# An attention layer on one Trainium2 core: sums of squares of four heads in fp32 in the array's column groups, roots on transposed sums, and two value chunks behind the first score blocks

## The chip, the cores and the metric

The kernel runs on one core of one Trainium2 chip. The core has five engines that matter here: TensorE, a 128 x 128 array for matrix products, written PE (its loads of stationary weights are shown apart, as PEld); VectorE, DVE; ScalarE, ACT; GpSimd, POOL; and SyncE, SP, which issues the DMAs. Matrix products are accumulated in PSUM, a memory of eight banks of 128 partitions x 512 fp32 numbers; everything else lies in SBUF.

The metric is device time in microseconds (us) of one execution, as the median of several runs.

## What is computed

The reference is a backbone of two layers over 512 latent tokens (width 1024) and 256 context tokens, in fp32. Layer 0 mixes with a gated convolution, layer 1 with attention; around each mixer stands a SwiGLU half step. The change is inside the attention mixer. Cut to it:

```python
D_MODEL, SEQ, CTX_LEN, HEAD_DIM = 1024, 512, 256, 128
N_HEADS, N_KV_HEADS, Q_BLOCK, NORM_EPS = 8, 2, 128, 1e-6

def rms_norm(x, g):
    return x * lax.rsqrt(jnp.mean(x * x, axis=-1, keepdims=True) + NORM_EPS) * g

def project_qkv(h, w_qkv, q_g, k_g):
    qkv = h @ w_qkv                      # 8 q heads, 2 k heads, 2 v heads
    ...
    return rms_norm(q, q_g), rms_norm(k, k_g), v

def gqa_block(q, k, v):
    s = jnp.einsum('bqkgd,bskd->bkgqs', q, k) * (HEAD_DIM ** -0.5)
    return jnp.einsum('bkgqs,bskd->bqkgd', jax.nn.softmax(s, axis=-1), v)

def attention_mixer(h_lat, h_ctx, ...):
    q_l, k_l, v_l = project_qkv(h_lat, w_qkv, q_g, k_g)
    q_c, k_c, v_c = project_qkv(h_ctx, w_qkv, q_g, k_g)
    q_l, k_l = apply_rope_2d(q_l, cos, sin), apply_rope_2d(k_l, cos, sin)
    k_all, v_all = concat(k_c, k_l), concat(v_c, v_l)     # 768 keys
    o_l = ...gqa_block over blocks of 128 queries...
    return o_l @ w_o
```

For every q head the kernel needs, per token, the root of the mean of 128 squares. Since this factor is the same for all keys, it isn't multiplied into q but given to the exponential of the softmax as its scale (rq), and to the row's maximum with a minus sign (nrq).

## The kernel before

**Products.** Activations lie transposed, features on partitions and tokens along the free dimension. An fp32 product is made of three products in a reduced type (fp32r): a number is split into a high part, a copy made by ACT, and a low part, the difference made by DVE (split, L179 to L181); mm3 (L808 to L811) forms high times high, high times low and low times high into one PSUM bank. Weights arrive by DMA as raw tiles and are split in the same way (w<-raw at L180 and L181), well ahead of their use; w_get takes the next split weights, w_done gives the space of those used back.

**Projections.** attention (from L1314) projects the heads one after the other. p is the projected head in PSUM (bank tag A, for head 2 tag B). A head's work behind its projection comes in two steps: q_head or k_head issues ACT's and DVE's part, and the function post that it returns issues the PE part, which is put into the middle of a later projection (behind, and the loop over the value chunks). For a q head (L1362) ACT squares p into hs; parts_of (L616 to L620) forms th, an ACT copy with epsilon added, and tl, the DVE difference; turned applies the rotary tables; post (L1369, L1370) multiplies pick, a matrix of zeros with one column of ones, with th and tl, so that the sum over the 128 partitions lands in row h of the 8 x 512 tile ps_Q. For a k head parts_of is followed by rstd_of, whose sums are broadcast over all partitions (ps_S).

**Value chunks.** Then six chunks of 128 tokens are multiplied by the v weights (loop over sc, L1423 to L1437), 24 products each, into one of two B banks; ACT copies the high parts vh and DVE forms the low parts vl, for each of the two kv heads g. Behind chunk 3 the 8 x 512 tile of sums gets its reciprocal root (rsqrt, L605 to L612: logarithm and exponential on ACT, one refinement step on DVE). Behind chunk 5 four transposes turn it into 128 x 32 (ps_S), and DVE writes rq and nrq.

**The block loop.** PSUM is then given out anew: C, two tiles of two banks each, for scores, T for transposes, O for the output. For each of 8 heads and 4 blocks of 128 queries: scores forms a 128 x 768 tile ps_C (six products), DVE its row maximum and the bias sm, ACT the exponential pr with its row sum, DVE the reciprocal, and the scaling of pr is done by DVE (even blocks) or ACT (odd blocks). turn makes six 128 x 128 transposes of pr, in two trios with a T tile each; ACT copies a trio into the high part of p and DVE forms the low part. values multiplies two blocks' p with the values into ps_O, which is split into o. The loop runs scores two blocks ahead of turn, and values one step behind. After block 15 T is given two banks instead of three, and one bank goes to the output projection of heads 0 to 3, whose steps (filler) fill the rest of the loop.

**What sets the order.** PE and SP run their instructions in the order in which the code issues them. For ACT and DVE a scheduler chooses the order when the program is built; on the chip each engine runs its instructions one by one in that order. Tiles of one tag share a ring of buffers: a new tile waits until the tile that held its buffer has been read for the last time.

Of the kernel before, what the change touches and what calls it, by code (L numbers as in the profile page):

```python
# [9 lines left out]
F32 = mybir.dt.float32  # L10
# [111 lines left out]
def backbone(ctx: ExitStack, tc: tile.TileContext, a: dict, out: bass.AP):  # L122
# [8 lines left out]
    def ctile(name, shape, dt=F32):  # L131
        return const.tile(shape, dt, name=name, tag=name)
# [13 lines left out]
    def ptile(name, shape=(P, 512)):  # L146
        pool, tag = bank[name]
        return pool.tile(list(shape), F32, name=f"ps_{name}", tag=tag)
# [13 lines left out]
    q_g, k_g = vec["attn_q_g"], vec["attn_k_g"]  # L162
    ones_r = ctile("ones_r", [P, P], F32R)
    dve.memset(ones_r.bitcast(F32), 1.0)
    pick = ctile("pick", [P, 2 * HEADS], F32R)
    dve.memset(pick.bitcast(F32), 0.0)
    dve.memset(pick[:, HEADS : HEADS + 1].bitcast(F32), 1.0)
    eps_t = {}
    for dim in (D, HD):
        eps_t[dim] = ctile(f"eps{dim}", [P, 1])  # L170
# [5 lines left out]
    def slot(n, shape, name, dt=F32R):  # L176
        return xp.tile([P, *shape], dt, name=name, tag=f"T{n}")
# [1140 lines left out]
    def attention(gp, i, s, after):  # L1318
# [7 lines left out]
        make_identity(nc, ident)  # L1326
        part_tiles[:] = (gp, "th"), (gp, "tl")

        with tc.tile_pool(name="rope", bufs=1) as rp, psum(A=4, B=2, S=1, Q=1):
            rope_c = rp.tile([P, NL], F32, name="rope_c", tag="rope_c")  # L1330
            rope_s = rp.tile([P, NL], F32, name="rope_s", tag="rope_s")
            pq = ptile("Q", (HEADS, NL))

            def turned(dst, p, g, n):

# [24 lines left out]
                return post  # L1360

            def q_head(p, h):  # L1362
                t = tmp.tile([P, NL], F32, name="hs", tag="t")
                act.activation(t, p, AF.Square)
                th, tl = parts_of(t, NL, HD)
                turned(qf[h], p, q_g, NL)

                def post():
                    pe.matmul(pq, pick[:, HEADS - h : 2 * HEADS - h], th, start=(h == 0), stop=False)  # L1369
                    pe.matmul(pq, pick[:, HEADS - h : 2 * HEADS - h], tl, start=False, stop=(h == HEADS - 1))  # L1370

                return post

# [46 lines left out]
            for h in range(3, HEADS):  # L1420
                q_project(h, 2 if 4 <= h < 7 else 1)
            wv = [w_get() for _ in range(4)]
            for sc in range(6):  # L1423
                post = heads.pop(0)() if heads else None
                p = ptile("B", (P, 2, 256))[:, 0, :]
                ts = slice(sc * P, (sc + 1) * P)
                for k in range(KC):
                    if post and k == KC // 2:
                        post()
                    wvh, wvl = (t[:, 2 * (k % 2) : 2 * (k % 2) + 2, :] for t in wv[k // 2])  # L1430
                    pe.matmul(p, hh[k][:, ts], wvh, start=(k == 0), stop=False)
                    pe.matmul(p, hl[k][:, ts], wvh, start=False, stop=False)
                    pe.matmul(p, hh[k][:, ts], wvl, start=False, stop=(k == KC - 1))
                for g in range(KVH):
                    pg = p[:, g * HD : (g + 1) * HD]
                    act.activation(vh[g][:, sc, :], pg, AF.Copy)
                    dve.tensor_tensor(out=vl[g][:, sc, :], in0=pg, in1=vh[g][:, sc, :].bitcast(F32), op=ALU.subtract)  # L1437
                if sc == 3:
                    r8 = tmp.tile([P, NL], F32, name="r8", tag="r", bufs=2)[:HEADS, :]
                    rsqrt(r8, pq, HEADS, NL, HD)  # L1440
            w_done()
            pt = ptile("S", (P, 4, HEADS))
            for b in range(4):
                pe.transpose(pt[:, b, :], r8[:, b * P : (b + 1) * P], ident[:HEADS, :HEADS])
            dve.tensor_scalar_mul(rq, pt, isq)
            dve.tensor_scalar_mul(nrq, pt, -isq)

        def o_tiles(g):

            got = []  # L1450
            for n in ((4, 5, 8), (11, 12, 13))[g]:
                t = slot(n, [3, NL], f"o{n}")
                got += [t[:, c, :] for c in range(3)]
            return got[:4], got[4:8]

        with tc.tile_pool(name="core", bufs=2) as cp, psum(C=2, O=1), ExitStack() as more:
            more.enter_context(psum(T=3))
            gates.append(lambda: gate_vec(i, s, False))
            st = {}

# [51 lines left out]
                split(oh[h % 4][:, hs], ol[h % 4][:, hs], p)  # L1512

            blocks = [(h, blk) for h in range(HEADS) for blk in range(4)]
            ready = [scores(*blocks[0]), scores(*blocks[1])]
            late = None
            filler = iter(())
            for n, (h, blk) in enumerate(blocks):
                if n + 2 < len(blocks):
                    ready.append(scores(*blocks[n + 2]))  # L1520
                p = turn(h, blk, ready[n])
                ready[n] = None
                if late:
                    values(*late)
                    if late[:2] == (3, 1):
                        more.close()
                        more.enter_context(psum(T=2, AB=1))
                        filler = out_steps(((0, NL),), None, *st["o"], 4, None, banks, 1)
                    late = None
                elif n > 16:  # L1530
                    next(filler, None)
                if blk % 2:
                    late = (h, blk // 2, *p)
# [282 lines left out]
```

## Time and profile before

| | us |
|---|---|
| three runs | 2478.07, 2478.75, 2479.18 (median 2478.75) |
| the profiled execution | 2477.58 |
| its span in the trace | 2475.8 |
| PE busy in the span | 2430.9 |
| DVE busy | 1891.7 |
| ACT busy | 1093.9 |
| block loop: first values product of block pair 0, and of pair 7 | at 1956.29 and 1998.25 |

The table's last row and all rows below are on the trace's own clock, which begins at the span's start. A row of the timeline reads: start, duration, engine, line of the kernel, operation, what it writes <- what it reads, shape, and, in brackets, how long the engine stood idle before it and what ended the wait. Matmuls are pipelined: the duration of one is longer than the distance to the next. DVE rows overlap a little as well, so the cost of one instruction in a stream is the distance between starts. "Pitch" below is that distance.

### The profile page before, as it was taken

The page shows a single profiled execution, that of the slowest core. Times are in us where ns is not written, and L with a number is a line of the kernel's source. Part 1 is how long each engine was busy: PE and PEld are TensorE (multiplying, and loading weights), DVE is VectorE, ACT ScalarE, POOL GpSimd, SP SyncE. Part 2 cuts the span into 40 slices and gives each one's busy share as a digit, 9 for nine tenths or more (in the row PEclk, how much of TensorE's full clock was granted, in tenths as well). Part 3 has the DMA queues.
Part 4 walks back from the last instruction along what each step waited for, and adds up shares of the span by engine and source line. Part 5 has one row for each costly group of instructions (what it writes and reads, how often), then busy time and mean ns, then how long its engine had stood idle before and what let it go on. Part 6 is the DMA issues. An engine that isn't in the chain of part 4 may idle for free.

```text
span 2475.8 us, 35587 instructions
## 1 busy us (share of the span) xinstructions
PE 2430.9 (98%) x13632; PEld 2261.2 (91%) x13632; DVE 1891.7 (76%) x3758; ACT 1093.9 (44%) x2018; POOL 7.1 (0%) x16
## 2 busy tenths in 40 slices
PE   6999999999999999999999999999999999999998
PEld 4899999999999999999999999999997899888887
DVE  4689879878988888878887978778878887544443
ACT  4443343355535643433445534334346775432233
POOL 0000000000000000000000000000000000000000
PEclk8999999999999999999999999999999999999999
DMA  7333433440333023423331234324332101333321
GB/s 266 111 124 116 129 127 119 128 145 18 107 92 121 19 97 125 129 85 123 127 118 42 78 110 156 117 90 151 122 111 69 35 18 60 103 102 95 101 77 35
DMA packets 107803, 253.58 MB, mean 102 GB/s; under 512 B 10224, under 2 KB 19568, under 8 KB 107632
## 3 DMA queue, kind: packets, MB, share of 16 engines
q1 hardware_dynamic: 105632, 245.92, 30.7%
q0 software_dynamic: 1152, 4.19, 0.5%
q8 instruction: 107, 1.75, 0.3%
q10 hardware_dynamic: 848, 1.18, 0.1%
q14 instruction: 64, 0.52, 0.1%
HBM read 249.16 MB, written 2.10 MB: 101 GB/s over the span
## 4 chain that ended last, share of the span: by engine, by line
PE 94%; DVE 2%; ACT 2%; DMA 1%; issue 0%; SPq 0%; DVEq 0%; ACTq 0%
PE ps_A L810 18%; PE ps_A L809 18%; PE ps_A L811 18%; PE ps_C L809 9%; PE ps_C L810 9%; PE ps_C L811 9%; PE ps_B L811 3%; PE ps_B L810 3%; PE ps_B L809 3%; PE ps_T L1496 1%; DMA ada<-in_ada_w 0%; ACT pr L1480 0%; PE ps_C L1473 0%; PE ps_O L809 0%; PE ps_O L811 0%
## 5 line engine op out<-in xcount | busy, mean ns | idle before, releaser
L180 ACT ACTIVATE w<-raw 128x512 fp32r<-128x512 f32 (+2 forms) x810 | 489.0, 618 | 744.7 <-PE ps_A L811 313.5
L181 DVE TENSOR_TENSOR w<-raw,w 128x512 fp32r<-128x512 f32 (+2 forms) x810 | 539.2, 677 | 187.6 <-ACT w L180 180.2
L810 PE MATMUL ps_A<-gl,w 128*128 128x512 f32 (+2 forms) x624 | 212.1, 340 | 0.4 <-DVE gl L181 0.4
L809 PE MATMUL ps_A<-gh,w 128*128 128x512 f32 (+2 forms) x624 | 211.7, 339 | 0.1
L811 PE MATMUL ps_A<-gh,w 128*128 128x512 f32 (+2 forms) x624 | 211.5, 339 | 0.0
L809 PE MATMUL ps_C<-gh,w 128*128 128x512 f32 (+1 forms) x472 | 165.4, 350 | 0.0
L875 DVE SCALAR_TENSOR_TENSOR x<-ps_A,gat,x 128x512 f32<-128x512 f32 (+1 forms) x192 | 118.8, 621 | 60.9 <-PE ps_A L811 60.3
L810 PE MATMUL ps_C<-gl,w 128*128 128x512 f32 (+1 forms) x472 | 165.3, 350 | 0.0
L811 PE MATMUL ps_C<-gh,w 128*128 128x512 f32 (+1 forms) x472 | 164.8, 349 | 0.0
L810 PE MATMUL ps_A<-hl,w 128*128 128x512 f32 (+1 forms) x424 | 162.1, 382 | 2.5 <-DVE hl L669 2.4
L809 PE MATMUL ps_A<-h,w 128*128 128x512 f32 (+1 forms) x424 | 161.6, 381 | 1.0 <-DVE x L875 1.0
L811 PE MATMUL ps_A<-h,w 128*128 128x512 f32 (+1 forms) x424 | 161.5, 381 | 0.0
L348 DVE TENSOR_TENSOR raw<-raw,raw 128x512 f32<-128x512 f32 x204 | 139.8, 688 | 26.2 <-DMA raw<-in_ffn_w_in 23.7
L875 DVE SCALAR_TENSOR_TENSOR x<-ps_C,gat,x 128x512 f32<-128x512 f32 (+1 forms) x136 | 87.8, 646 | 68.6 <-PE ps_C L811 68.4
L810 PEld LDWEIGHTS ps_A<-gl,w 128*128 128x128 f32 x624 | 118.3, 190 | 15.8 <-DVE gl L181 1.9
L809 PEld LDWEIGHTS ps_A<-gh,w 128*128 128x128 f32 x624 | 118.3, 190 | 15.2 <-ACT gh L180 1.0
L811 PEld LDWEIGHTS ps_A<-gh,w 128*128 128x128 f32 x624 | 118.3, 190 | 12.7
L809 PE MATMUL ps_A<-tB11h,w 128*128 128x384 f32 x312 | 106.8, 342 | 2.4 <-ACT tB11h L764 2.4
L810 PE MATMUL ps_A<-tB11l,w 128*128 128x384 f32 x312 | 106.2, 340 | 0.3 <-DVE tB11l L766 0.3
L811 PE MATMUL ps_A<-tB11h,w 128*128 128x384 f32 x312 | 105.9, 340 | 0.0
L811 PEld LDWEIGHTS ps_C<-gh,w 128*128 128x128 f32 x472 | 89.3, 189 | 11.8
L811 PE MATMUL ps_C<-tB22h,w 128*128 128x384 f32 x296 | 100.0, 338 | 0.0
(425 smaller groups left out, 6526.1 us busy)
## 6 DMA issues: line engine op xcount, KB each, us to landing
raw<-in_ffn_w_in SPq DMA_DIRECT2D x174, 512.0 KB, 3.7
aw<-in_ada_t SPq DMA_DIRECT2D x240, 256.0 KB, 2.7
raw<-in_ffn_w_out SPq DMA_DIRECT2D x76, 512.0 KB, 4.0
raw<-in_conv_w_in SPq DMA_DIRECT2D x24, 512.0 KB, 3.6
ada<-in_ada_w SPq DMA_DIRECT2D x27, 256.0 KB, 5.9
raw<-in_attn_w_qkv SPq DMA_DIRECT2D x12, 512.0 KB, 4.8
crow<-in_c_rows POOLq DMA_DIRECT2D x8, 512.0 KB, 4.9
raw<-in_ada_w SPq DMA_DIRECT2D x8, 512.0 KB, 5.1
```

The lines of the kernel that those rows point to most:

```text
L180: act.activation(dsth, src, AF.Copy)
L181: dve.tensor_tensor(out=dstl, in0=src, in1=dsth.bitcast(F32), op=ALU.subtract)
L348: dve.tensor_tensor(out=quad(o), in0=quad(x), in1=quad(y), op=ALU.subtract)
L809: pe.matmul(ps, wh, xh, start=first, stop=False, **kw)
L810: pe.matmul(ps, wh, xl, start=False, stop=False, **kw)
L811: pe.matmul(ps, wl, xh, start=False, stop=last, **kw)
L875: dve.scalar_tensor_tensor(out=x, in0=p[:, o - off : o - off + w], scalar=gat[:, m, v : v + 1], in1=x, op0=ALU.mult, op1=ALU.add)
L1496: pe.transpose(pt[:, c, :], pr[:, (c0 + c) * P : (c0 + c + 1) * P], ident)
```

## The change

**Sums of squares.** pick becomes an fp32 matrix of 33 columns, with ones in column 1. Each q head's squares stay in a buffer of their own (qs, four of them, one for each head of a group of four); th and tl are no longer formed for q heads. Behind head 3 and behind head 7 four fp32 products of 32 x 512 are issued, one for each head of the group, each into another group of 32 columns of the array and so into another 32 partitions of ps_Q: the sum lands in row 32 g + 0 for head g, in row 32 g + 1 for head 4 + g.

**Roots.** Behind chunk 2 ACT copies all 128 rows of ps_Q (sums). Behind chunk 3 four 128 x 128 transposes turn them; DVE picks the eight useful columns out of each and adds epsilon (each), and the root is formed on 128 x 32 numbers, with the tokens on partitions.

**Value chunks and banks.** Chunks 4 and 5 move into the block loop's beginning, behind the scores of blocks 0 and 1. The PSUM tags B (2 banks), S and Q live on through the loop: T shares the two B banks, O takes Q's, the filler's A takes S's. C takes the four banks that A had in the projections.

```diff
-    pick = ctile("pick", [P, 2 * HEADS], F32R)
-    dve.memset(pick.bitcast(F32), 0.0)
-    dve.memset(pick[:, HEADS : HEADS + 1].bitcast(F32), 1.0)
+    pick = ctile("pick", [P, 33])
+    dve.memset(pick, 0.0)
+    dve.memset(pick[:, 1:2], 1.0)
...
-        with tc.tile_pool(name="rope", bufs=1) as rp, psum(A=4, B=2, S=1, Q=1):
+        with psum(B=2, S=1, Q=1), ExitStack() as core:
+            early = ExitStack()
+            rp = early.enter_context(tc.tile_pool(name="rope", bufs=1))
+            early.enter_context(psum(A=4))
...
-            pq = ptile("Q", (HEADS, NL))
+            pq = ptile("Q")
+            squares = []
...
             def q_head(p, h):
-                t = tmp.tile([P, NL], F32, name="hs", tag="t")
+                t = rp.tile([P, NL], F32, name="qs", tag=f"qs{h % 4}")
+                squares.append(t)
                 act.activation(t, p, AF.Square)
-                th, tl = parts_of(t, NL, HD)
                 turned(qf[h], p, q_g, NL)

                 def post():
-                    pe.matmul(pq, pick[:, HEADS - h : 2 * HEADS - h], th, start=(h == 0), stop=False)
-                    pe.matmul(pq, pick[:, HEADS - h : 2 * HEADS - h], tl, start=False, stop=(h == HEADS - 1))
+                    row, last = divmod(h, 4)
+                    if last < 3:
+                        return
+                    for g in range(4):
+                        pe.matmul(pq[32 * g : 32 * g + 32, :], pick[:, 1 - row : 33 - row], squares[4 * row + g], start=(row == 0), stop=(row == 1), tile_position=(0, 32 * g), skip_group_check=True)
...
-            for sc in range(6):
+
+            def value_chunk(sc):
...
-                if sc == 3:
-                    r8 = tmp.tile([P, NL], F32, name="r8", tag="r", bufs=2)[:HEADS, :]
-                    rsqrt(r8, pq, HEADS, NL, HD)
-            w_done()
-            pt = ptile("S", (P, 4, HEADS))
+            for sc in range(3):
+                value_chunk(sc)
+            sums = tmp.tile([P, NL], F32, name="r8", tag="r", bufs=2)
+            act.activation(sums, pq, AF.Copy)
+            value_chunk(3)
+            pt = ptile("S", (P, 4, P))
             for b in range(4):
-                pe.transpose(pt[:, b, :], r8[:, b * P : (b + 1) * P], ident[:HEADS, :HEADS])
-            dve.tensor_scalar_mul(rq, pt, isq)
-            dve.tensor_scalar_mul(nrq, pt, -isq)
...
-        with tc.tile_pool(name="core", bufs=2) as cp, psum(C=2, O=1), ExitStack() as more:
-            more.enter_context(psum(T=3))
+                pe.transpose(pt[:, b, :], sums[:, b * P : (b + 1) * P], ident)
+            each = tmp.tile([P, 4, HEADS], F32, name="each", tag="each", bufs=1)
+            dve.tensor_scalar_add(each.rearrange("p b (c g) -> p b c g", g=4), pt.rearrange("p b (g c) -> p b c g", g=4)[:, :, :2, :], EPS * HD)
+            flat = [t.rearrange("p b h -> p (b h)") for t in (nrq, each)]
+            rsqrt(*flat, P, 4 * HEADS, HD)
+            dve.tensor_scalar_mul(rq, nrq, isq)
+            dve.tensor_scalar_mul(nrq, nrq, -isq)
...
+            early.close()
+            bank["T"], bank["O"] = bank["B"], bank["Q"]
+            cp = core.enter_context(tc.tile_pool(name="core", bufs=2))
+            core.enter_context(psum(C=2))
...
-            ready = [scores(*blocks[0]), scores(*blocks[1])]
+            ready = [scores(*blocks[0])]
+            value_chunk(4)
+            ready.append(scores(*blocks[1]))
+            value_chunk(5)
+            w_done()
...
                     if late[:2] == (3, 1):
-                        more.close()
-                        more.enter_context(psum(T=2, AB=1))
+                        bank["A"] = bank["S"]
```

How this moves instructions is shown at three places, first on PE where the sum of head 3 stood, in the projection of a later head (h and hl are the two parts of the layer's normed input, w its split weights, ps_A the bank of the projection); "-" is before, "+" the change.

```order
 L810 MATMUL ps_A<-hl_17602,w_17969 128x512
 L811 MATMUL ps_A<-h_17601,w_17969 128x512
-L1369 MATMUL ps_Q<-th,pick 8x512
-L1370 MATMUL ps_Q<-tl,pick 8x512
+L1377 MATMUL ps_Q<-qs,pick 32x512 x4
 L809 MATMUL ps_A<-h_17611,w_17969 128x512
 L810 MATMUL ps_A<-hl_17612,w_17969 128x512
```

The pair of products on th and tl is replaced by four on the squares themselves; for heads 0 to 2 and 4 to 6 the pair is gone with nothing in its place.

The second place is the beginning of the block loop on ACT. First the rows before: vh_17657 and vh_17658 are the high parts of a chunk's values for the two kv heads, L1480 is the exponential of a block, L1483 the scaling of an odd block, p the copy of a trio of transposes.

```order
L1436 ACTIVATE vh_17657<-ps_B 128x128
L180 ACTIVATE qh<-qf_17747 128x512
L180 ACTIVATE w_19242<-raw_18092 128x512
L1436 ACTIVATE vh_17658<-ps_B 128x128
L1480 ACTIVATE pr,sm<-ps_C,sm,rq 128x768 x2
L1483 ACTIVATE pr<-pr,sm 128x768
L180 ACTIVATE p_18569<-ps_T 128x3x128
L1480 ACTIVATE pr,sm<-ps_C,sm,rq 128x768
L180 ACTIVATE p_18569<-ps_T 128x3x128 x3
```

And the same place of the change, from the last weight copies ahead of the exponential of block 1 on (L1496 is the exponential now, L1499 the scaling, L1444 the copy of values):

```order
L180 ACTIVATE w_19186<-raw_18080 128x512
L1496 ACTIVATE pr,sm<-ps_C,sm,rq 128x768
L1444 ACTIVATE vh_17657<-ps_B 128x128
L180 ACTIVATE w_19189<-raw_18080 128x512
L1499 ACTIVATE pr<-pr,sm 128x768
L180 ACTIVATE p_18523<-ps_T 128x3x128
L1444 ACTIVATE vh_17658<-ps_B 128x128
L1496 ACTIVATE pr,sm<-ps_C,sm,rq 128x768
L180 ACTIVATE p_18523<-ps_T 128x3x128
```

Chunk 5's two copies stand now behind the exponential of block 1, the second one behind the first trio of block 0. On DVE the same place of the change reads so (L1493 is the maximum of a block, L1494 its bias, L1497 the reciprocal of a row sum, L1445 the low parts vl of a chunk; T is p's source):

```order
L1497 RECIPROCAL sm<-sm 128x1
L1493 TENSOR_REDUCE sm<-ps_C 128x1
L1445 TENSOR_TENSOR vl_17659<-ps_B,vh_17657 128x128
L1494 TENSOR_TENSOR sm<-sm,nrq 128x1
L181 TENSOR_TENSOR w_19189<-raw_18080,w_19189 128x512
L181 TENSOR_TENSOR p_18524<-ps_T,p_18523 128x3x128
L1445 TENSOR_TENSOR vl_17660<-ps_B,vh_17658 128x128
L1493 TENSOR_REDUCE sm<-ps_C 128x1
```

The last vl of chunk 5 has moved from ahead of the first maximum to behind the maximum of block 2, the split of a weight and the low part of the first trio.

The third place is one round of the loop on ACT in heads 0 to 3. Before:

```order
L180 ACTIVATE p_18705<-ps_T 128x3x128
L1480 ACTIVATE pr,sm<-ps_C,sm,rq 128x768
L180 ACTIVATE p_18705<-ps_T 128x3x128
L1483 ACTIVATE pr<-pr,sm 128x768
L1480 ACTIVATE pr,sm<-ps_C,sm,rq 128x768
L180 ACTIVATE o_18642<-ps_O 128x256
L180 ACTIVATE qh<-qf_17748 128x512
```

In the change:

```order
L1496 ACTIVATE pr,sm<-ps_C,sm,rq 128x768
L180 ACTIVATE p_18659<-ps_T 128x3x128 x2
L1499 ACTIVATE pr<-pr,sm 128x768
L1496 ACTIVATE pr,sm<-ps_C,sm,rq 128x768
L180 ACTIVATE o_18596<-ps_O 128x256
L180 ACTIVATE qh<-qf_17748 128x512
L180 ACTIVATE p_18659<-ps_T 128x3x128 x2
```

The exponential of an even block now stands ahead of both copies of the trios, not between them.

More of the change, by code (lines that the diff above doesn't have):

```diff
@@ L1437, in attention, with o_tiles @@
                     dve.tensor_tensor(out=vl[g][:, sc, :], in0=pg, in1=vh[g][:, sc, :].bitcast(F32), op=ALU.subtract)
-                if sc == 3:
-                    r8 = tmp.tile([P, NL], F32, name="r8", tag="r", bufs=2)[:HEADS, :]
-                    rsqrt(r8, pq, HEADS, NL, HD)
-            w_done()
-            pt = ptile("S", (P, 4, HEADS))
-            for b in range(4):
-                pe.transpose(pt[:, b, :], r8[:, b * P : (b + 1) * P], ident[:HEADS, :HEADS])
-            dve.tensor_scalar_mul(rq, pt, isq)
-            dve.tensor_scalar_mul(nrq, pt, -isq)
[L1448 to L1454, printed above, removed]
-        with tc.tile_pool(name="core", bufs=2) as cp, psum(C=2, O=1), ExitStack() as more:
-            more.enter_context(psum(T=3))
+            for sc in range(3):
[4 more added lines that the diff above has]
+            pt = ptile("S", (P, 4, P))
+            for b in range(4):
+                pe.transpose(pt[:, b, :], sums[:, b * P : (b + 1) * P], ident)
[5 more added lines that the diff above has]
+            dve.tensor_scalar_mul(nrq, nrq, -isq)
+            def o_tiles(g):
+                got = []
+                for n in ((4, 5, 8), (11, 12, 13))[g]:
+                    t = slot(n, [3, NL], f"o{n}")
+                    got += [t[:, c, :] for c in range(3)]
+                return got[:4], got[4:8]
+            early.close()
+            bank["T"], bank["O"] = bank["B"], bank["Q"]
+            cp = core.enter_context(tc.tile_pool(name="core", bufs=2))
+            core.enter_context(psum(C=2))
             gates.append(lambda: gate_vec(i, s, False))
```

## The prediction

> **What bounds the kernel now.** I read the page's busy shares first, then its chain of work that ended last, then the windows of the attention stage, and last the timeline inside each window.
>
> ```profile
> PE 2430.9 (98%) x13632; PEld 2261.2 (91%) x13632; DVE 1891.7 (76%) x3758; ACT 1093.9 (44%) x2018; POOL 7.1 (0%) x16
> PE 94%; DVE 2%; ACT 2%; DMA 1%; issue 0%; SPq 0%; DVEq 0%; ACTq 0%
> 1890.00:1925.00 35.00, 31.81 (x139) 24.00 (x138) 32.49 (x57) 27.32 (x51) 0.00 (x0) 1.00 0.25 76
> 1945.20:1948.66 3.46, 1.21 (x8) 0.87 (x6) 3.05 (x7) 1.26 (x5) 0.00 (x0) 1.00 0.39 136
> 1948.66:1952.08 3.42, 3.28 (x13) 2.99 (x13) 1.90 (x4) 2.31 (x5) 0.00 (x0) 0.50 0.43 153
> ```
>
> TensorE (PE) is busy for 98% of the span and 94% of the chain lies on it, so only two things move the end: work taken from PE, and idle time of PE. A window row gives the stretch, its length, the busy time of PE, weight load, VectorE (DVE), ScalarE (ACT) and GpSimd, then the granted clock. The first window is the projection of the q and k heads: PE stands 35.00 − 31.81 = 3.19 us, and DVE, with 32.49 of 35.00 busy, has almost nothing to spare. The other two are the seam between the value chunks and the block loop: PE works 1.21 of 3.46 us, and then for 3.42 us at a granted clock of 0.50.
>
> **Term 1, the sums of squares.** The first pair of rows runs from the last sum on head 6 to the next projection matmul; the others are fp32 column-group products of another part of the program, the nearest rows there are to the new ones.
>
> ```profile
> 1922.56 0.39 PE L1369 MATMUL ps_Q<-th,pick 128*8 128x512 f32 x1
> 1923.02 0.39 PE L809 MATMUL ps_A<-h,w 128*128 128x512 f32 x1
> 38.24 0.34 PE L811 MATMUL ps_C<-tB11h,w 128*128 128x384 f32 x1
> 38.51 1.07 PE L472 MATMUL ps_B<-ada,silu_p 128*32 128x512 f32 x8
> 39.79 0.34 PE L810 MATMUL ps_A<-tB11l,w 128*128 128x384 f32 x1
> 39.97 0.34 PE L811 MATMUL ps_A<-tB11h,w 128*128 128x384 f32 x1
> 46.62 0.63 PE L472 MATMUL ps_B<-ada,silu_p 128*32 128x512 f32 x3
> 47.07 0.60 PE L472 MATMUL ps_B<-ada,silu_p 128*32 128x512 f32 x3
> ```
>
> A pair of sums holds PE for 1923.02 − 1922.56 = 0.46 us (the first row is the th product, its tl follows). Eight pairs go: 8 × 0.46 = 3.7. What comes is two bursts of four. Eight such products between 38.24 and 39.79 took 1.55, of which two are pitches of an ordinary matmul (39.97 − 39.79 = 0.18 each), so about 1.2 for eight; a following group adds 47.07 − 46.62 = 0.45. One burst of four thus lies between 0.45 and 1.2. I take 0.75, two bursts 1.5, with the ends 0.9 and 2.4. Net gain 2.2 (1.3 to 2.8). The memset of 33 columns instead of 16 is at the program's start, beside the first loads, and counts as nothing; if that cover were gone it is one short DVE instruction.
>
> **Term 2, the waits in the projection.** Each row's bracket gives the idle time ahead and who ended it.
>
> ```profile
> 1899.60 0.40 PE L1370 MATMUL ps_Q<-tl,pick 128*8 128x512 f32 x1 [0.97 <-DVE tl L620]
> 1906.88 0.40 PE L1370 MATMUL ps_Q<-tl,pick 128*8 128x512 f32 x1 [0.60 <-DVE tl L620]
> 1916.65 0.40 PE L1369 MATMUL ps_Q<-th,pick 128*8 128x512 f32 x1 [1.23 <-ACT th L619]
> 1917.44 0.41 PE L1370 MATMUL ps_Q<-tl,pick 128*8 128x512 f32 x1 [0.39 <-DVE tl L620]
> L620 DVE SCALAR_TENSOR_TENSOR tl<-hs,eps,th x12: 476/745/753, 1883.0 to 1931.4; 128x512 fp32r<-128x512 f32 x10, 128x256 fp32r<-128x256 f32 x2
> 1908.07 0.48 DVE L620 SCALAR_TENSOR_TENSOR tl<-hs,eps,th 128x256 fp32r<-128x256 f32 x1
> 1909.33 0.28 PE L627 MATMUL ps_S<-tl,ones_r 128*128 128x256 f32 x1
> ```
>
> All 3.19 us of idle time in that window stand ahead of sums on q heads: 0.97 + 0.60 + 1.23 + 0.39. A broken stream also shows 0.39 instead of a pitch of 0.23 (half a pair) at the end of each of the four, 0.16 each: 3.84 in all. In the change the sums of heads 0 to 2 are not there, and the burst behind head 3 reads squares that were written a projection earlier, so these four waits go.
>
> What is late next is DVE. It is 93% busy here; PE loses 3.84 plus its own share of the sums (five pairs of the eight in this window, 2.3, less one burst), about 5.4, while DVE loses five tl of 0.745 each (about 0.66 as pitch, since each starts before the one ahead has ended), 3.3. So of 3.84 between all and 3.84 − 2.1 = 1.7 stays. Walking along the remaining sums, those on the k heads: the tl of 1908.07 comes three tl earlier (2.0), while PE's matmul of 1909.33, which now stands 0.78 behind the end of that tl, would come 0.97 + 0.60 + two times 0.16 + three pairs (1.4) = 3.3 earlier. It waits again, 3.3 − 2.0 − 0.78 = 0.5, with the 0.16 of a broken stream 0.7; for the second k head, which DVE forms right behind, I take 0.4, an estimate. Term 2 gives 3.84 − 1.1 = 2.7 (1.7 to 3.84). The four transposes on 128 rows stand in for four on 8 rows; the roots stand beside chunk 4. Both at nothing; without that cover the root's chain, seven short instructions of some 0.2 (the reciprocal's row below has 0.16), would be one more wait of about 1.4 us ahead of the second exponential.
>
> **Term 3, the seam.** Rows in order: a chunk's first and last row of the last step, the start of scores 0, the end of scores 1, where PE resumes, the first values product, and the one seven pairs of blocks later.
>
> ```profile
> 1940.75 0.28 PE L1431 MATMUL ps_B<-w,h 128*128 128x256 f32 x1
> 1943.49 0.28 PE L1433 MATMUL ps_B<-w,h 128*128 128x256 f32 x1
> 1944.04 0.50 PE L1473 MATMUL ps_C<-kh,qh 128*128 128x512 f32 x1
> 1946.13 0.28 PE L1475 MATMUL ps_C<-kh,ql 128*128 128x256 f32 x1
> 1948.80 0.80 PE L1473 MATMUL ps_C<-kh,qh 128*128 128x512 f32 x1 [2.39 <-ACT pr L1480]
> 1956.29 0.36 PE L809 MATMUL ps_O<-p,vh 128*128 128x256 f32 x1
> 1998.25 0.37 PE L809 MATMUL ps_O<-p,vh 128*128 128x256 f32 x1
> 1959.56 0.82 PE L1496 MATMUL ps_T<-ident,pr 128*128 128x128 f32 x6
> 1960.13 0.48 PE L1473 MATMUL ps_C<-kh,qh 128*128 128x512 f32 x1
> ```
>
> From scores 0 to the first values product pass 12.25 us. The work in it is five score blocks of about 1.1 (two end 0.12 after the start of the row at 1946.13, 2.21 behind 1944.04) and six trios of transposes of about 0.28 (1960.13 − 1959.56 = 0.57 for two), 7.2. So 12.25 − 7.2 = 5.0 is there to gain. Two chunks of 2.86 each (1943.49 − 1940.75 + 0.12) now come between, and with them a stall at a new place. Let s be the start of scores 0: chunk 4 ends at s + 4.0, scores 1 at 5.1, chunk 5 at 7.9, scores 2 at 9.0, the first trio of block 0 at 9.3. The second trio needs a bank; the two that it may have are those of chunks 4 and 5, and chunk 5's is free only when DVE has formed the last vl. In the new ACT order the first trio's copy stands behind the exponential and the scaling of block 1, which begin after chunk 5 has taken DVE's weight splits with it: exponential at 7.9, a vh of 0.28 and a weight copy of 0.6, scaling done at 10.5, the copy at 11.0. DVE, whose maximum of block 2 waits for scores 2 until 9.0 and is followed by a vl, the bias and a weight split, comes to p at 11.0 as well, ends it at 11.5, and only then forms vl, to 11.8. PE stands 9.3 to 11.8, **2.5 us**. Behind it: trio 12.1, scores 3 13.2, trio 13.5, a wait of 1.4 for its partner's bank (a maximum of 0.87 and a p of 0.55 on DVE), trio 15.2, scores 4 16.3, two trios 16.9: the first values at s + 17.0. Less the 5.7 of the chunks that is 11.3, against 12.25: a gain of 1.0. Its bounds are 5.0 (no wait at all) and −0.6 (the clock halves again, below). The weights of the chunks are given back some 6 us later, and the loads behind them with that; I cost it at nothing, since those are first used behind block 16, 42 us later (1998.25 − 1956.29); what would show otherwise is an idle PE ahead of the output projection.
>
> **Term 4, heads 0 to 3 with two transpose banks instead of three.** These rows are one round of the loop on ACT and DVE.
>
> ```profile
> 1967.59 0.99 ACT L1480 ACTIVATE pr<-ps_C,sm,rq 128x768 f32<-128x768 f32 x1 [0.59 <-DVE sm L1478]
> 1968.57 0.86 ACT L180 ACTIVATE p<-ps_T 128x384 fp32r<-128x384 f32 x2
> 1970.24 0.97 ACT L1480 ACTIVATE pr<-ps_C,sm,rq 128x768 f32<-128x768 f32 x1
> 1971.34 0.16 DVE L1481 RECIPROCAL sm<-sm 128x1 f32<-128x1 f32 x1 [0.39 <-ACT pr L1480]
> 1972.40 0.95 DVE L1477 TENSOR_REDUCE sm<-ps_C 128x1 f32<-128x768 f32 x1
> 1973.73 0.15 DVE L1478 TENSOR_TENSOR sm<-sm,nrq 128x1 f32<-128x1 f32 x1
> 1952.12 0.16 DVE L1478 TENSOR_TENSOR sm<-sm,nrq 128x1 f32<-128x1 f32 x1
> 1952.37 0.99 ACT L1480 ACTIVATE pr<-ps_C,sm,rq 128x768 f32<-128x768 f32 x1
> ```
>
> With three banks a transpose ring runs ahead of its copies; with two, and ACT's order now exponential, two copies, scaling, exponential, the chain of this round closes on itself: exponential to its row sum and reciprocal, scaling, the split of o, maximum, a p, the bias of the next exponential. From 1967.59 to 1973.73 are 6.14, and from the bias to its exponential 1952.37 − 1952.12 = 0.25: 6.39 a pair of blocks. PE's pair is now (1998.25 − 1956.29) / 7 = 5.99. The difference is 0.40; over six pairs, blocks 4 to 16, a loss of 2.4 (0, if the copies still run ahead, to 8.7, below). Heads 4 to 7 have two banks on both sides.
>
> **The sum.** 2.2 + 2.7 + 1.0 − 2.4 = 3.5 us. The profiled execution took 2477.58 (span 2475.8), 1.17 below the median of 2478.75 and 0.49 below the lowest of the three runs; taken from the median: **2475.2 us**, 0.14% faster. About 0.2%, or 5.0 us, is what a measurement of this kernel can tell from no change.
>
> **The rivals.**
> R1, the new stall halves the clock too. For: the 2.39 us stall did, and the window behind it shows 0.50. Against: the new one ends with PE busy just ahead of it. Price: half of 3.28 busy us, 1.6: 2476.8.
> R2, the chunks cover the seam fully (5.0 in place of 1.0): 2471.2. For: chunk 5 gives DVE 2.86 us more. Against: the order of ACT and DVE at that place, which runs in line. If only the ring costs nothing, 2472.8.
> R3, the change doesn't do what it says: the removed waits come back whole behind the k heads, because DVE bounds the projection. Term 2 becomes 0: 2477.9. For: 32.49 of 35.00 busy. Against: DVE sheds 3.3 us too.
> R4, slower: PE waits in each pair for two copies and a scaling on ACT, where it now waits for one copy: 1970.24 − 1968.57 = 1.67, less half of the 0.86 that two copies take, 1.24 a pair over seven pairs, 8.7 in place of 2.4: 2481.5. It turns the sign from 5.9 / 7 = 0.84 a pair. For: two banks leave no lead. Against: block pairs of 5.99 leave PE's products of values, some 2 us, between the two trios.
>
> The Trainium skill, page "TensorE: Matmul & The Clock Gate", section "Why this matters for your kernels", asks for no idle gaps of TensorE over about 3 us between bursts, since one costs the half clock. By that rule neither the 2.39 us stall nor the new one halves the clock, and R1 falls to nothing; the window row with 0.50 behind 2.39 us says otherwise, and the measurement decides. With the rule the sum would be 2475.2, with the row's price 2476.8.
>
> **How the numbers follow.** Forecast 0.38; R1 0.17; R2 0.17, with the free ring a further 0.10; R3 0.09; R4 0.09. The range leaves out R4 and the far tails: 2470.6 to 2478.2. Faster by over 0.2% needs 2473.8 or less: R2 and the free ring, 0.27, and a fifth of the forecast, 0.07, make 0.34. Slower by over 0.2% is the half of R4 that meets R1 or R3 as well, 0.05. The rest, 0.61, is within 0.2%.
>
> **What would show it.** In the profile after: two bursts at L1377 of 0.45 to 1.2 us each and no idle time ahead of them (term 1 and 2); a wait on tl ahead of the sums of the k heads under 1 us (term 2; over 2 us is R3); one PE stall of 2 to 3 us that a vl ends behind chunk 5 (term 3; none is R2), and the clock behind it (R1); a pair of blocks of heads 0 to 3 at 6.4 us (term 4; 6.0 frees the ring, 7.2 is R4). Wrong would be the whole sum if scores 0 starts less than 2 us or over 8 us earlier.

## The result, and the profile after

| | before | the change |
|---|---|---|
| median of 4 runs, us | 2478.41 (2476.12 to 2479.18) | 2454.65 (2452.30 to 2455.11) |
| ratio to before | | 0.9905, 95% interval 0.9893 to 0.9917 |
| profiled execution, span, us | 2477.58, 2475.8 | 2454.45, 2452.6 |

The change takes off 23.8 us, 0.96%, where 3.5 were forecast: below the range. First the page's busy line and the line of the chain by engine, then the attention stage of the change.

```profile
PE 2404.7 (98%) x13632; PEld 2240.6 (91%) x13632; DVE 1881.5 (77%) x3751; ACT 1087.6 (44%) x2011; POOL 7.1 (0%) x16
PE 90%; DVE 5%; ACT 3%; DMA 1%; issue 1%; SPq 0%; DVEq 0%; ACTq 0%
```

PE has as many matmuls as before and is busy for 26.2 us less (2430.9 − 2404.7). The removed idle time was not the point: PE's idle time grew from 44.9 to 47.9. The same window of the fourth quarter, which ends ahead of the attention stage and so of every edited product, of the kernel before and then of the change:

```profile
1600.00:1800.00 200.00, 200.00 (x1144) 192.38 (x1143) 157.13 (x307) 77.04 (x143) 0.00 (x0) 1.00 0.37 119
```
```profile
1600.00:1800.00 200.00, 200.00 (x1155) 192.34 (x1154) 157.36 (x309) 79.53 (x150) 0.00 (x0) 1.00 0.40 128
```

Both are full and both have a granted clock of 1.00, yet the change gets 11 matmuls more into 200 us, 1%. So matmuls follow each other faster. The timeline of PE at 900 us, before and in the change, shows by how much:

```profile
900.04 0.34 PE L809 MATMUL ps_A<-tB11h,w 128*128 128x384 f32 x1
900.23 0.34 PE L810 MATMUL ps_A<-tB11l,w 128*128 128x384 f32 x1
900.40 0.34 PE L811 MATMUL ps_A<-tB11h,w 128*128 128x384 f32 x1
900.58 0.34 PE L809 MATMUL ps_A<-tB11h,w 128*128 128x384 f32 x1
900.75 0.34 PE L810 MATMUL ps_A<-tB11l,w 128*128 128x384 f32 x1
900.92 0.34 PE L811 MATMUL ps_A<-tB11h,w 128*128 128x384 f32 x1
```
```profile
899.97 0.33 PE L809 MATMUL ps_A<-tT2h,w 128*128 128x384 f32 x1
900.14 0.33 PE L810 MATMUL ps_A<-tT2l,w 128*128 128x384 f32 x1
900.32 0.33 PE L811 MATMUL ps_A<-tT2h,w 128*128 128x384 f32 x1
900.49 0.33 PE L809 MATMUL ps_A<-tT2h,w 128*128 128x384 f32 x1
900.66 0.33 PE L810 MATMUL ps_A<-tT2l,w 128*128 128x384 f32 x1
900.84 0.33 PE L811 MATMUL ps_A<-tT2h,w 128*128 128x384 f32 x1
```

Five distances take 0.88 before (900.92 − 900.04) and 0.87 in the change; in the trace's nanoseconds the first are 182, 176, 173, 174 and 175, after which 182 comes again, mean 176.0, and the second stay at 173 and 174. Over some 7,250 such matmuls 2.6 ns each are 19 us.

The places of the prediction, in the change: a burst between its neighbours, the wait at a k head's sum, scores 0, the two stalls, the first values product, the one seven pairs later, and the clock in the window behind the first stall.

```profile
1895.57 0.39 PE L811 MATMUL ps_A<-h,w 128*128 128x512 f32 x1
1895.89 1.07 PE L1377 MATMUL ps_Q<-qs,pick 128*32 128x512 f32 x8
1896.88 0.50 PE L809 MATMUL ps_A<-h,w 128*128 128x512 f32 x1
...
1889.51 0.39 PE L627 MATMUL ps_S<-tl,ones_r 128*128 128x256 f32 x1 [1.27 <-DVE tl L620]
...
1916.86 0.48 PE L1489 MATMUL ps_C<-kh,qh 128*128 128x512 f32 x1
...
1928.42 0.55 PE L1512 MATMUL ps_T<-ident,pr 128*128 128x128 f32 x3 [2.08 <-DVE p L181]
...
1931.70 0.30 PE L1512 MATMUL ps_T<-ident,pr 128*128 128x128 f32 x1 [1.34 <-DVE p L181]
...
1933.69 0.36 PE L809 MATMUL ps_O<-p,vh 128*128 128x256 f32 x1
...
1977.59 0.36 PE L809 MATMUL ps_O<-p,vh 128*128 128x256 f32 x1
```
```profile
1928.42:1931.80 3.38, 2.04 (x13) 1.70 (x14) 1.88 (x5) 2.36 (x5) 0.00 (x0) 1.00 0.43 156
```

Nearly everything that was forecast for these places is there, some of it with other sizes. What the forecast lacks lies outside them.

### The profile page after: what moved, and what is told of

Same layout as the page of the kernel before. It is cut to its first block, busy times and chain, and to the rows that moved or that the text cites. A ratio compares the mean times of both kernels' runs of the same rounds, so it can differ in the third digit from the quotient of the medians.

```text
span 2452.6 us, 35558 instructions
## 1 busy us (share of the span) xinstructions
PE 2404.7 (98%) x13632; PEld 2240.6 (91%) x13632; DVE 1881.5 (77%) x3751; ACT 1087.6 (44%) x2011; POOL 7.1 (0%) x16
## 4 chain that ended last, share of the span: by engine, by line
PE 90%; DVE 5%; ACT 3%; DMA 1%; issue 1%; SPq 0%; DVEq 0%; ACTq 0%
PE ps_A L810 17%; PE ps_A L809 17%; PE ps_A L811 17%; PE ps_C L809 9%; PE ps_C L810 9%; PE ps_C L811 9%; PE ps_B L811 3%; PE ps_B L810 3%; PE ps_B L809 3%; ACT pr L1496 1%; DVE f L742 1%; DMA ada<-in_ada_w 0%; DVE w L181 0%; PE ps_T L1512 0%; DVE x L875 0%
## 5 line engine op out<-in xcount | busy, mean ns | idle before, releaser
L809 PEld LDWEIGHTS ps_C<-gh,w 128*128 128x128 f32 x472 | 89.4, 189 | 12.1 <-issue 1.2
L811 PEld LDWEIGHTS ps_C<-gh,w 128*128 128x128 f32 x472 | 89.3, 189 | 11.8
```

Of the source, the lines that this page charges most:

```text
L809: pe.matmul(ps, wh, xh, start=first, stop=False, **kw)
L811: pe.matmul(ps, wl, xh, start=False, stop=last, **kw)
```

## The experiments

### Do start addresses in SBUF, all moved together, do it? (e1 to e4)

The wider pick moves every later SBUF tile up by 96 bytes. e1, e3 and e4 move the kernel before by 96, 32 and 64 bytes, e2 the change by 32.

```diff
     pick = ctile("pick", [P, 2 * HEADS], F32R)
+    dve.memset(ctile("pad", [P, 24]), 0.0)    # e1; 8 in e3, 16 in e4; in e2 8, behind the change's pick
```

> The kernel before, with one unused tile of 24 numbers behind pick, so that every later SBUF tile starts 96 bytes higher, at the same place modulo 128 as in the change (where the wider pick has done it); nothing else differs. Theory A (the start addresses in SBUF set the distance between matmuls): the 384-wide products come down from a mean of 0.176 to 0.1734 us, the 512-wide ones on h from 0.231 to 0.227, and the time to 2478.4 - 20 = about 2458, between 2455 and 2461. Theory B (the sums, the seam or the new banks bring the 24 us): 2478, as before. Theory C (something of the other day or chip): before and this alike.

> The change, with an unused tile of 8 numbers behind pick, so that later tiles start at 32 modulo 64 bytes again, as in the kernel before. Theory A: the distances between matmuls go back to 0.176 and 0.231, and the time to 2454.7 + 20 = about 2475, which is what the edits by themselves are worth (forecast 2475.2). Theory B: 2454.7, as the change.

> The kernel before, moved by 32 bytes: tiles start at 64 modulo 128. Theory A with a grain of 64 bytes: as e1, about 2458. Theory A with a grain of 128 bytes: slow still, about 2478, or between the two. Theory B: 2478.

> The kernel before, moved by 64 bytes: tiles start at 96 modulo 128, which is 32 modulo 64 as before. It has the same unused tile and memset as e1 and e3. Theory A with a grain of 64 bytes: no change, 2478. If the tile or its memset mattered and not the address, it would be as fast as e1.

Below, a kernel near 2478 us is called slow and one near 2454 fast. Measured: e1 2478.99 (ratio 1.0005, 0.9996 to 1.0014), e3 2478.72, e4 2477.80, all as before; e2 2453.73 (0.9903, 0.9890 to 0.9917), as the change. Theory A falls as it was put: a common shift does nothing. So does C, since all ran in turn on one chip.

### Which part of the change brings it? (e5 to e7)

e5 takes the sums alone: the change's q_head, pick and pq, its squares' buffers and, at sc == 3, its transposed roots with the tile each. e6 takes the seam and the bank plan alone, with the sums as before (the core of each edit against before and against the change):

```diff
-            for sc in range(6):
+            for sc in range(6):    # e5
...
+                if sc == 2:
+                    act.activation(sums, pq, AF.Copy)
+                if sc == 3:
...
```
```diff
-            act.activation(sums, pq, AF.Copy)    # e6
+            rsqrt(r8, pq, HEADS, NL, HD)
             value_chunk(3)
-                pe.transpose(pt[:, b, :], sums[:, b * P : (b + 1) * P], ident)
+                pe.transpose(pt[:, b, :], r8[:, b * P : (b + 1) * P], ident[:HEADS, :HEADS])
```
```diff
-    pick = ctile("pick", [P, 2 * HEADS], F32R)
+    pick = ctile("pick", [P, 64], F32R)    # e7
```

> The kernel before with the column-group sums, the transposed roots and the squares' own buffers, but with all six value chunks ahead of the loop and three transpose banks. All theories share the terms for the edits: sums 2.2 and waits 2.7, so 4.9 us, and about 2473 if the distances between matmuls all over the program stay as before (0.176 for 384 columns). Theory D (the sums on th and tl, in fp32r with 8 columns, are what slows matmuls everywhere, and taking them out is enough): 0.1734 everywhere and about 2454. Theory E (it comes with the seam or the bank plan): 2473.

> The change with the sums of before (th and tl, 8 x 512, root on 8 rows behind chunk 2, four transposes of 8 rows behind chunk 3): only the two chunks' place and the bank plan are the change's. Edits alone: seam +1.0 gain less 2.4 for the two-bank ring, so about 2480. Theory D: distances as before, 2480. Theory E: 0.1734 everywhere, about 2460.

> The kernel before with 32 instead of 8 columns in the weights of the sums (the rows behind the eighth are zero and not read): same count and order of instructions on every engine. If a stationary operand of 8 columns is what does it (Theory D in its narrow form): 0.1734 everywhere, about 2458. If it is the count or the order of instructions: as before, 2478.

Measured: e5 2451.87 (0.9899, 0.9884 to 0.9913), e6 2480.56 (1.0013, 1.0003 to 1.0022), e7 2477.46. The seam and the banks cost 0.7 to 5.5 us by that interval, where 1.4 was forecast, and bring no faster matmuls; whatever does comes in with the sums, and it is not the 8 columns.

### What in the sums? (e8 to e11)

```diff
-                    pe.matmul(pq, pick[:, HEADS - h : 2 * HEADS - h], th, start=(h == 0), stop=False)
-                    pe.matmul(pq, pick[:, HEADS - h : 2 * HEADS - h], tl, start=False, stop=(h == HEADS - 1))
+                    pe.matmul(pq, pick[:, HEADS - h : 2 * HEADS - h], t, start=(h == 0), stop=(h == HEADS - 1))    # e8, fp32
```
```diff
                 act.activation(t, p, AF.Square)    # e5's q_head
+                parts_of(t, NL, HD)    # e9
```
```diff
+        for q in range(9):    # e10, on e5, at the last stage
+            act.activation(dummy[:, q : q + 1], eps_t[D], AF.Copy)
+        for q in range(9, 23):
+            dve.memset(dummy[:, q : q + 1], 0.0)
```
```diff
+                    if h % 4 == 3:    # e11, on before
+                        spare = ptile("S")
+                        for g in range(4):
+                            pe.matmul(spare[32 * g : 32 * g + 32, :], pick2[:, 0:32], rope_c, start=True, stop=True, tile_position=(0, 32 * g), skip_group_check=True)
```

> The kernel before with one fp32 product of 8 columns per head on the squares, in place of two fp32r products on th and tl, which are not formed (epsilon is left out of the sum of squares in this kernel). No column groups, no transposed roots. If the absence of th and tl (two fp32r products a head, ACT and DVE work) is what sets the distances between matmuls all over the program: 0.1734 and about 2455. If the column groups do it: 0.176 and about 2475.

> The sums alone (e5), with th and tl of the q heads still formed by ACT and DVE and read by nobody. If ACT's and DVE's work is what does it: 0.176 and about 2475. If it is PE's part (column groups, fp32 in place of fp32r): 0.1734 and 2452 to 2456 (waits of the projection may come back with DVE's work).

> The sums alone (e5), with 9 tiny ACT copies and 14 tiny DVE memsets at the start of the last stage, so that both engines' programs are about as long as before's. If the length of these programs (where instructions lie in memory) sets the distances: 0.176 and about 2475. If not: 2452, as e5.

> The kernel before, whole, with two more bursts of four fp32 column-group products of 32 x 512 behind heads 3 and 7, written to a bank that nobody reads. If such bursts by themselves leave PE in a state in which matmuls follow each other at 0.1734: about 2478 + 1.5 - 22 = 2457. If not: 2478 + 1.5 = 2480, and the bursts' rows give their price.

Measured: e8 2479.23 and e11 2480.23 (1.0011), slow; e9 2450.92 and e10 2453.91, fast. Neither th and tl nor ACT's and DVE's work nor their programs' length nor column-group bursts by themselves do it. e11's two bursts add 2.4 to the median, near the 2.2 that two bursts of 1.08 take.

### Rows, SP's program, PE's program (e12 to e17)

```diff
+                if sc == 1:    # e12: 4 on e5; e16: 2 on before; e17: 1 on e5
+                    spare = ptile("S", (P, 4, HEADS))
+                    for b in range(4):
+                        pe.transpose(spare[:, b, :], rope_c[:HEADS, b * P : (b + 1) * P], ident[:HEADS, :HEADS])
```
```diff
-                pe.transpose(pt[:, b, :], r8[:, b * P : (b + 1) * P], ident[:HEADS, :HEADS])
+                pe.transpose(pt[:, b, :], r8[:128, b * P : (b + 1) * P], ident[:128, :128])    # e13; 32 in e14
```
```diff
+            dve.memset(rp.tile([P, 4 * NL], F32, name="room", tag="room")[:, :1], 0.0)    # e15, on before
```

> The sums alone (e5) with four transposes of 8 rows added behind chunk 1, written to the bank ps_S and read by nobody. Theory H (a product with an 8-row operand anywhere in the program sets longer distances between matmuls in all of it): 0.176 for 384 columns everywhere and about 2475. Theory I (the longer program of SP, 1143 instead of 1142 instructions, which all fast kernels share and this one has too): 0.1734 and about 2452.5.

> The kernel before with its four transposes on 128 rows instead of 8 (the other rows are set to zero first), nothing else: sums on th and tl, seam and banks as before, SP's program unchanged. Theory H: 0.1734 everywhere and 2478 - 20 = about 2457. Theory I: 0.176 and 2478.

> As e13 with 32 rows. Theory H, if any operand of fewer than 128 rows does it: 0.176 and 2478. If only fewer than 32 rows do: 0.1734 and about 2457. Theory I: 2478.

> The kernel before with an unused tile of 8 KB in the pool of the rotary tables, which moves these tables and gives SP the one more wait that the change has. Theory I: 0.1734 everywhere and about 2457. Theory H: 0.176 and 2478.

> The kernel before with two 8-row transposes added behind chunk 1, read by nobody, so that PE's program has 27388 instructions instead of 27383; nothing else. Theory L (the length of PE's program decides: of the programs run, those with 27380, 27385 and 27393 instructions, 0 or 1 modulo 4, were fast all over, those with 27378, 27379, 27383 and 27415, 2 or 3 modulo 4, slow): 27388 is 0 modulo 4, so 0.1734 for 384 columns from the first 200 us on, and about 2457. Theory M (something in the new sums or roots themselves, such as ACT's and DVE's instructions on 8 rows, which all slow kernels have): 0.176 and 2478.

> The sums alone (e5) with one such transpose, 27387 instructions instead of 27385, 3 modulo 4. Theory L: 0.176 for 384 columns, 0.231 for 512, and about 2452 + 21 = 2473, which is what the sums are worth by themselves (4.9 forecast). Theory M: 2452.

Measured: e12 2453.12 and e17 2452.36, fast; e13 2476.52, e14 2477.68, e15 2477.40 and e16 2478.50, slow. H, I and L all fall: every kernel descended from the new sums is fast, every other slow, whatever was added.

### Two operands' addresses, one against the other (e18)

The profiles at hand hold the answer once their matmuls are sorted by operands. For each matmul of 384 or 512 columns that is followed by one of the same width, take the distance of the two starts in the trace, less the bare one (173.3 or 226.7 ns, the usual distance in the fast kernels), and group by the difference between the SBUF start addresses of moving and stationary operand, modulo 256, that the programs name. Distances that a wait lengthens, by some 25 ns or more, are left out:

```
kernel   columns  difference  count   mean ns over the bare distance
before     384        0          47       0.50
before     384      128        7205       2.68
before     512        0        1876       0.93
before     512      128        1264       5.90
e1         384      128        7208       2.68
e1         512      128        1257       5.90
change     384        0        7251       0.08
change     512        0        3137       0.79
e18        384        0        7249       0.09
e18        512        0        3129       0.80
e10        384        0        7159       0.07
e10        384       96          92       3.35
e10        512        0        2717       0.93
e10        512       96         423       6.78
```

Inside the kernel before both kinds stand side by side: most of its 512-wide products on gh, which lies in the same region as the weights, are fast, and most of those on h slow. It is the difference that decides and not the operand: 176 products on h with a difference of 0 show 0.5 ns, 580 with 128 show 6.0; of those on gh, 1057 with 0 show 0.7 and 118 with 128 show 5.7. In all twelve programs that take 2476 us or more (before, e1, e3, e4, e6 to e8, e11, e13 to e16; e18's expectation counts them as ten) the activations of 7296 or more 384-wide products and of 1300 or more 512-wide ones start 128 from their weights. In the seven that take 2455 or less (the change, e2, e5, e9, e10, e12, e17) they start level with them modulo 256, save 528 products of e10, which differ by 96, since its unused tile of 96 bytes moves the last stage's activations, and are slow one by one. Where one operand starts does not decide: of most 384-wide products, before and e18 (below) have the activations at 32 modulo 256, and before and e2 have the weights at 160; each time one of the two is slow and the other fast. The change's small tile each, of 128 bytes, is in the pool tmp, which lies between the activations' pool and the weights'. In e1 to e4 both moved together. e18 is the kernel before with that one move:

```diff
                 if sc == 3:
+                    dve.memset(tmp.tile([P, 4, HEADS], F32, name="each", tag="each", bufs=1), 0.0)
                     r8 = tmp.tile([P, NL], F32, name="r8", tag="r", bufs=2)[:HEADS, :]
```

> The kernel before with one unused tile of 128 bytes in the pool tmp (the size and the pool of the change's tile each), which lies between the activations' pool and the weights' pool: weights, raw tiles and all that lies behind them start 128 bytes higher, activations, vectors and tmp where they were. Nothing else differs but one memset. Theory R (what counts is the distance between the start addresses of the two operands of a matmul, activations against weights, modulo 256: it is 128 in all ten slow programs and 0 in all seven fast ones, and inside the kernel before itself the 512-wide products with a distance of 0 show 0.9 ns over the bare 226.7 and those with 128 show 5.9): 0.1734 for 384 columns, 0.227 for h, and 2477 - 20 = about 2457, between 2453 and 2460. Theory M (the new sums or roots themselves): 0.176 and 2478.

Measured: 2454.19 against 2478.23 in the same session, ratio 0.9903 (0.9887 to 0.9920). A tile that nobody reads takes off 24.0 us, as much as the whole change, in a kernel that has none of the new sums and roots: theory M falls, and R stands. Its window of the fourth quarter, and its scores 0 and its values products:

```profile
1600.00:1800.00 200.00, 200.00 (x1155) 192.34 (x1154) 158.48 (x310) 81.20 (x151) 0.00 (x0) 1.00 0.40 129
```
```profile
1927.85 0.50 PE L1474 MATMUL ps_C<-kh,qh 128*128 128x512 f32 x1
...
1938.69 0.36 PE L809 MATMUL ps_O<-p,vh 128*128 128x256 f32 x1
...
1980.69 0.36 PE L809 MATMUL ps_O<-p,vh 128*128 128x256 f32 x1
```

The table gives its size too: 7205 × 2.68 + 1264 × 5.90 + 1876 × 0.93 ns is 28.5 us, less the change's 7251 × 0.08 + 3137 × 0.79, 3.1: 25.4, against 24.0 measured.

## Why the prediction was wrong, by its own steps

**The step that failed** is the first: "only two things move the end: work taken from PE, and idle time of PE". The sum had no term for the matmuls that stay. It took the distances between them as fixed, and costed the edits' tiles at nothing beside their instructions; a 128-byte tile between two pools gave 24 us. Its own sign of being wrong showed: scores 0 starts 1944.04 − 1916.86 = 27.2 us earlier than before, 21.5 without the two chunks that now come behind it, and not 2 to 8. The page showed nothing of it: 98% busy and clock 1.00 looked like a limit, while the rows of one shape, 0.176 here and 0.1734 in the change, were not at it. The prediction's 512-wide pitch of 0.23 was the slow one; two digits hid it, since by the table it was 0.2326 before and is 0.2275 in the change.

**The edits by themselves** are seen against e18, which has the change's addresses and none of its edits; both traces stand at the same time ahead of the stage, in a row of ps_A on h at 1838.59 in the change and 1838.57 in e18.

- Terms 1 and 2, 4.9 forecast: scores 0 starts at 1916.86 against 1927.85, two chunks (5.7) earlier in the work: 1927.85 − 1916.86 − 5.7 = **5.3**. Of that, 1.6 is not the edits' doing: behind two waits at a q head's sums e18's clock is halved for a while (rows below), and nine pitches take 1904.21 − 1900.56 = 3.65 where 9 × 0.227 = 2.04 would do. The change has neither the waits nor the half clock there, and the kernel before had the waits and kept 1.00 (the prediction's first window). So the edits gave 3.7. A burst takes 1.08 (1896.88 − 1895.57 less a pitch of 0.23), not 0.75, within its bounds, so the sums gave 1.5, not 2.2. That leaves 2.2 for the waits, where 2.7 was forecast: the projection waits once, 1.27 at a k head, where 1.1 was forecast for two. R3 is out.
- Term 3, +1.0: from scores 0 to the first values product 1933.69 − 1916.86 − 5.7 = 11.1, forecast 11.3, with stalls of 2.08 and 1.34 where 2.5 and 1.4 were forecast. The mechanism is right. Against the kernel before (12.25) it gains 1.1, but against e18 it loses **0.3**: e18 needs only 1938.69 − 1927.85 = 10.84, since its stall doesn't halve the clock. The gain was in the clock and not in the cover, R2 is out, and R1 is as well: 1.00 in the window behind the new stall.
- Term 4, −2.4: seven pairs take 1977.59 − 1933.69 = 43.90, 6.27 each, against 42.00 in e18. **−1.9**; steady pairs take 6.32, forecast 6.39. R4 is out.

```profile
1898.77 0.40 PE L1369 MATMUL ps_Q<-th,pick 128*8 128x512 f32 x1 [1.26 <-ACT th L619]
1899.63 0.40 PE L1370 MATMUL ps_Q<-tl,pick 128*8 128x512 f32 x1 [0.47 <-DVE tl L620]
```
```profile
1900.50:1904.30 3.80, 3.80 (x11) 2.93 (x11) 3.51 (x7) 3.71 (x7) 0.00 (x0) 0.55 0.00 0
```

These make 5.3 − 0.3 − 1.9 = 3.1 of the 3.5 forecast, and the values product of the last pair starts 3.10 earlier in the change than in e18 (2040.18 against 2043.28). Against the kernel before, whose half clock lies at the seam, inside the 12.25, they make 3.7 + 1.1 − 1.9 = 2.9. In either sum about half is a half clock that the other kernel has and the change has not, and that is luck: without it the edits stand at 3.7 − 0.3 − 1.9 = 1.5. Then two things come that the prediction doesn't have. The rows are the change's, on ACT, DVE and PE at the loop's end, and a window behind a stall that both kernels have:

```profile
2039.69 3.24 ACT L180 ACTIVATE oheld<-raw 128x512 fp32r<-128x512 f32 x6 [1.53 <-PE ps_A L811]
...
2042.84 0.36 ACT L180 ACTIVATE o<-ps_O 128x256 fp32r<-128x256 f32 x1
...
2043.45 0.41 DVE L181 TENSOR_TENSOR o<-ps_O,o 128x256 fp32r<-128x256 f32 x1
...
2043.92 0.39 PE L809 MATMUL ps_A<-o,oheld 128*128 128x256 f32 x1 [1.43 <-DVE o L181]
...
2073.95 0.51 PE L810 MATMUL ps_A<-hl,w 128*128 128x256 f32 x1 [2.14 <-DVE hl L669]
```
```profile
2073.90:2077.30 3.40, 3.35 (x16) 3.35 (x17) 3.38 (x9) 2.29 (x7) 0.00 (x0) 0.52 0.43 130
```

PE waits 1.43 for the last split of ps_O, which stands behind six weight copies on ACT; with the broken stream that is 1.6 (2043.92 − 2042.21 less a pitch of 0.12). e18 has the same order on ACT and no such wait, and e6, the seam and banks alone, has it with 1.45: it comes with the bank plan. The program's bank numbers offer the reason, which was not tried apart: O now lies in Q's bank, the fourth, and the next stage's four A banks are the first four; before, O was not among them. And behind the 2.14 us stall, which both have, the change's clock is 0.52 and e18's 1.00 (below), which costs 1.1. 3.1 − 1.6 − 1.1 = 0.4 are left; with neither kernel's half clock counted, 1.5 − 1.6 = −0.1. The medians, 2454.65 and 2454.19, can't tell that from nothing.

So the edits are worth about nothing in the end: by themselves they gave 1.5 against e18 up to the loop's end, and a wait that the forecast lacks took that back. The 24 us are the tile's. e5, the sums without the seam and the bank plan, has 2451.87 (2450.68 to 2453.76), the lowest of those timed more than twice, some 2.8 below the change; the intervals of their ratios overlap.

## What to carry to other kernels

Before bounding a stage by "PE is busy", compare the distance between matmuls of one shape across the program: where the same shape has two distances, or a repeating pattern, PE is busy and not at its limit. A tile put into a pool between activations and weights can be a change of every wide matmul: hold operand addresses fixed when an edit is judged, or try the edit's bare tile alone, as e18 does. And where a change is far larger than its parts, look first at a window that it doesn't touch.

## What the runs showed of the hardware that was not expected

- Wide matmuls depend on where their two operands lie against each other: with start addresses 128 bytes apart modulo 256 they take 2.7 ns (384 columns) and 5.9 ns (512) over the bare distance, with 0 some 0.1 and 0.8, in every kernel whose matmuls were sorted so; 256-wide ones don't lose (0.120 us with 0 and 0.119 with 128, in the kernel before). 96 bytes apart, in e10, they take as much or more, 3.35 and 6.78. Other differences than 0, 96 and 128 were too rare to tell. That the two reads disturb each other is a possible reason, and no run here shows it.
- Stalls of the same length do or don't halve the granted clock behind them, and shorter ones can: the waits of 1.26 and 0.47 in e18's projection did, and 1.23 and 0.39 at the same place in the kernel before did not. The rows below are first e18's stall at its seam (2.40), 1.00 behind it, where the kernel before had 2.39 and 0.50; then its 2.14 stall, 1.00, where the change has 0.52:

```profile
1932.34:1935.80 3.46, 3.19 (x22) 2.93 (x23) 2.75 (x7) 3.10 (x7) 0.00 (x0) 1.00 0.48 152
2075.34:2078.70 3.36, 3.30 (x24) 3.07 (x25) 3.34 (x9) 2.28 (x7) 0.00 (x0) 1.00 0.45 136
```

The Trainium skill, page "TensorE: Matmul & The Clock Gate", section "Part 1: The HAM clock gate (the "warmup" mystery)", says that activity is watched in a window that runs freely, and that the point at which the clock changes depends on where in that window the first matmul lands. The rows are in keeping with that, though no run here moves a stall against the window on purpose: it is a matter of 1.1 to 1.6 us either way that no edit controls here.
